# Moving the half-size Strassen step of a feed-forward chunk pair from the front of the chunk to its middle

## The chip, the cores and the metric

The kernel runs on one core of one Trainium2 chip. The metric is the device time of one execution in microseconds (us); less is better. The kernel before was run three times: 2200.41, 2201.24 and 2201.27 us, median 2201.24. The engines are named as in the profile: PE does matrix products (PEld is its weight load), DVE and ACT do element-wise work on 128-partition tiles, SP issues the transfers from device memory (HBM), and POOL does a few small things.

## The reference, cut to what matters

One decoder layer over 256 tokens of 2048 channels, all in float32. Two SwiGLU feed-forward blocks (FFN1 and FFN2, inner width 5504) stand around a mixer; the change touches only the first product of each feed-forward block.

```python
def swiglu(x, w_in, w_out):
    a, u = jnp.split(x @ w_in, 2, axis=-1)
    return (jax.nn.silu(a) * u) @ w_out

x = layer_norm(ALPHA * x + 0.5 * swiglu(x, ffn1_w_in[i], ffn1_w_out[i]), ln_g[i, 0], ln_b[i, 0])
...
x = layer_norm(ALPHA * x + 0.5 * swiglu(x, ffn2_w_in[i], ffn2_w_out[i]), ln_g[i, 2], ln_b[i, 2])
```

## The kernel before, in words

**Three passes.** A float32 product is made of three PE matrix products: weights and activations are each split into a high part and a remainder, and high x high (L1210), then high x remainder and remainder x high (both L1214) are added up in one PSUM bank. For the weights, ACT casts the loaded tile to its high part `wh` (L1141) and DVE subtracts it to get the remainder `wl` (L1153). One such pair (`wh`, `wl`) covers two k-tiles (a k-tile is 128 of the 2048 input channels) by 512 columns. In the feed-forward blocks there is room for six pairs (`NMAIN`). A pair is free again when PE has used it for the last time, so casts, and the splits behind them, can run at most six pairs ahead of PE.

**Chunk pairs.** In a feed-forward block, column chunk number 2 to 10 of the gate half and the same chunk of the up half make one `Quad`: two token tiles times two column slabs. With a low and a high block of k-tiles the four blocks of weights are called 11 (low k, gate), 12 (low k, up), 21 (high k, gate) and 22 (high k, up). A Quad takes k-tiles 0 to 7 by a Strassen-Winograd form with seven products in place of eight. It goes in two full steps: step 0 with low k-tiles 0, 1 and high 4, 5, and step 1 with 2, 3 and 6, 7. Each full step is seven elements: `11`, `t1`, `22`, `t3`, `t2`, `21`, `t4` (written `11.0` for step 0 and `11.1` for step 1). The four `t` elements are sums of weight blocks, added in place on DVE before the cast (L1119). Each element is one pair and serves two products, six matrix products on PE.

**The short step.** Chunks 2 to 9 of each feed-forward block (16 Quads, form "short") also take k-tile 8 as low and k-tile 9 as high by the same seven products: elements `h1`, `h2`, `h3`, `h4`. Their buffers are half as deep per block: `h1` reads a buffer of ring 11 that holds 11 and 22 side by side, `h2` is the sum of that buffer and a ring 21 buffer (12 and 21 side by side) written to a ring 12 buffer, `h3` is a half-size add, `h4` another. The k-tiles 10 to 15 are done plainly: elements `a0`..`a2` (gate) and `u0`..`u2` (up), each one pair that serves four products. Chunk 10 is a Quad of form "long" without a short step.

**Output units.** Between Quads stand two plain output units (`w_out` of the chunks of the group before), four pairs each; I call their eight pairs o1 to o8. Each pair serves four products.

**Rings.** Plain weight tiles come through a ring of four buffers (`raw`). The Strassen blocks come through rings of their own: two buffers for 11, one each for 12, 21 and 22 (`HIGH`). All loads go through SP's queue in one fixed order; a load waits there until its buffer is free. Ring 21's single buffer is freed by the add of `t4` (which takes the block 21 in) and, for the short step, by the split of `h4`. Ring 12's is freed by the splits of `t3` and of `h2`. `may_load` says which ring may load; its test on `shorted` keeps ring 12 empty until `h2` has been written to it.

**What sets the order.** `Quad.ORDER` (L87) is the order of a Quad's elements by hand: PE's products, the adds, casts and splits all follow it, through `feed` (L1166). When the program is built, a scheduler may move an instruction ahead of others on its engine, by its own estimate of when operands are ready; from then on every engine runs its list strictly as it stands. The number of PSUM banks for accumulation in these stages is seven (a Quad uses `p1` to `p7`).

Of the kernel before, what the change touches and what calls it, by code (L numbers as in the profile page):

```python
# [66 lines left out]
class Quad:  # L67
# [17 lines left out]
    SHORT = (8, 9)  # L85
    PLAIN = ((10, 11), (12, 13), (14, 15), (8, 9))
    ORDER = {  # L87
# [55 lines left out]
def hybrid_layer(ctx: ExitStack, tc: tile.TileContext, x, p, ln_g, ln_b, ffn1_w_in, ffn1_w_out, mix_w_in,  # L143
# [883 lines left out]
    for u in units:  # L1027
# [3 lines left out]
        if isinstance(u, Quad):  # L1031
            base = len(plan)
            for el in u.els:
# [3 lines left out]
                for key, ks, slab in el.get("load", ()):  # L1037
                    ring = key[2] if key else "raw"
                    if not key:
                        key = el["src"] = len(plan)  # L1040
# [43 lines left out]
    def may_load(ring):  # L1084
        if not loads[ring]:
            return False
        if ring == "raw":
            return taken["raw"] < NRAW
        key, kind = loads[ring][0][:2]
        if ring == "12" and not key[0].shorted:  # L1090
            return False
        return kind == region["kind"] and held["on"] and (held[ring] < HIGH[ring] or key in half)

# [72 lines left out]
    def feed():  # L1166
        while True:
            ring = min((r for r in loads if may_load(r)), key=lambda r: first_use[loads[r][0][0]], default=None)
            if ring:
                weight_dma(ring)  # L1170
            elif addable():
                weight_add()
            elif castable():
                weight_cast()
            elif cur["split"] < cur["cast"]:
                weight_split()
            else:
                return
# [141 lines left out]
```

## Time and profile before

| what | value |
|---|---|
| median of three runs | 2201.24 us |
| the profiled execution's own time | 2200.81 us |
| its span, first to last instruction | 2199.1 us |
| DVE busy | 1827.5 us (83%) |
| ACT busy | 1182.8 us (54%) |
| weight splits on DVE (L1153) | 975 instructions, 1140.9 us |
| weight casts on ACT (L1141) | 975 instructions, 975.9 us |
| weight adds on DVE (L1119) | 216 instructions, 254.7 us |
| granted PE clock | 0.998 over the span |

The span is what lies between the first and the last instruction; the execution's own time is 1.71 us more. "Busy" is a share over stages with different limits, so the stage of the change has to be looked at by itself. In a row of the timeline the first number is the start in us, the second the length, and a bracket at the end gives how long the engine was idle before the row and what it then waited for. A PE row's end is modelled: rows of 0.39 us that start 0.23 us apart are a full pipeline. Equal rows that follow each other are merged with a count, and then the length runs from the first start to the last end.

### The profile page before, as it was taken

The page shows a single profiled execution, that of the slowest core. Times are in us where ns is not written, and L with a number is a line of the kernel's source. Part 1 is how long each engine was busy: PE and PEld are TensorE (multiplying, and loading weights), DVE is VectorE, ACT ScalarE, POOL GpSimd, SP SyncE. Part 2 cuts the span into 40 slices and gives each one's busy share as a digit, 9 for nine tenths or more (in the row PEclk, how much of TensorE's full clock was granted, in tenths as well). Part 3 has the DMA queues.
Part 4 walks back from the last instruction along what each step waited for, and adds up shares of the span by engine and source line. Part 5 has one row for each costly group of instructions (what it writes and reads, how often), then busy time and mean ns, then how long its engine had stood idle before and what let it go on. Part 6 is the DMA issues. An engine that isn't in the chain of part 4 may idle for free.

```text
span 2199.1 us, 27091 instructions
## 1 busy us (share of the span) xinstructions
PE 2175.5 (99%) x9996; PEld 1811.4 (82%) x9996; DVE 1827.5 (83%) x2066; ACT 1182.8 (54%) x1412; POOL 20.0 (1%) x48
## 2 busy tenths in 40 slices
PE   9999999999999999999999999999999999999997
PEld 7988888888887888888888888798888888888886
DVE  6899999999886678657898888779999989998667
ACT  5555555555555534534565554645555555555463
POOL 1000000000000000000000000000000000000000
PEclk9999999999999999999999999999999999999999
DMA  8866666566663665554665676566666666665564
GB/s 263 265 193 200 210 204 194 186 201 211 208 194 116 197 216 178 185 181 153 220 203 177 202 244 210 171 210 201 192 200 189 203 211 201 201 210 176 192 221 144
DMA packets 228245, 436.29 MB, mean 198 GB/s; under 512 B 14608, under 2 KB 23312, under 8 KB 228112
## 3 DMA queue, kind: packets, MB, share of 16 engines
q1 hardware_dynamic: 226832, 430.37, 61.7%
q0 software_dynamic: 1280, 4.20, 0.5%
q8 instruction: 78, 1.28, 0.2%
q14 instruction: 55, 0.45, 0.1%
HBM read 430.31 MB, written 4.19 MB: 198 GB/s over the span
## 4 chain that ended last, share of the span: by engine, by line
PE 95%; DVE 2%; DMA 1%; ACT 1%; issue 1%; SPq 0%; DVEq 0%; ACTq 0%
PE bank L1214 61%; PE bank L1210 31%; PE bank L289 2%; PE bank L694 1%; DVE wl L1153 1%; DMA raw<-in_ffn_w_in_dram 1%; ACT wh L1141 1%; DMA raw<-in_ffn_w_out_dram 0%; DVE x L510 0%; DVE x L511 0%; PE bank L664 0%; ACT yT L490 0%; DVE x L496 0%; DVE raw L1119 0%; DVE bn L430 0%
## 5 line engine op out<-in xcount | busy, mean ns | idle before, releaser
L1141 ACT CAST wh<-raw 128x1024 fp32r<-128x1024 f32 (+2 forms) x975 | 975.9, 1030 | 763.0 <-PE bank L1214 331.3
L1153 DVE TENSOR_TENSOR wl<-raw,wh 128x1024 fp32r<-128x1024 f32 (+2 forms) x975 | 1140.9, 1197 | 237.1 <-ACT wh L1141 224.4
L1214 PE MATMUL bank<-wh,xl 128*128 128x512 f32 (+1 forms) x1624 | 625.6, 386 | 2.8 <-DVE xl L303 1.9
L1214 PE MATMUL bank<-wl,xh 128*128 128x512 f32 (+1 forms) x1624 | 625.9, 386 | 0.4 <-DVE wl L1153 0.4
L1210 PE MATMUL bank<-wh,xh 128*128 128x512 f32 (+1 forms) x1624 | 616.0, 387 | 0.4 <-ACT xh L302 0.4
L1214 PEld LDWEIGHTS bank<-wh,xl 128*128 128x128 f32 x1624 | 304.9, 188 | 63.3 <-DVE xl L303 4.0
L1210 PEld LDWEIGHTS bank<-wh,xh 128*128 128x128 f32 x1624 | 304.9, 188 | 58.9 <-ACT xh L302 1.5
L1214 PEld LDWEIGHTS bank<-wl,xh 128*128 128x128 f32 x1624 | 305.0, 188 | 58.6 <-DVE wl L1153 1.4
L1214 PE MATMUL bank<-wl,gh 128*128 128x512 f32 x896 | 348.5, 391 | 2.3 <-DVE wl L1153 2.3
L1214 PE MATMUL bank<-wh,gl 128*128 128x512 f32 x896 | 347.9, 390 | 0.0
L1210 PE MATMUL bank<-wh,gh 128*128 128x512 f32 x896 | 345.7, 392 | 0.0
L1119 DVE TENSOR_TENSOR raw<-raw,raw 128x1024 f32<-128x1024 f32 x216 | 254.7, 1180 | 12.4 <-DMA raw<-in_ffn_w_in_dram 6.7
L1214 PEld LDWEIGHTS bank<-wl,gh 128*128 128x128 f32 x896 | 168.3, 188 | 39.0 <-DVE wl L1153 4.8
L1210 PEld LDWEIGHTS bank<-wh,gh 128*128 128x128 f32 x896 | 168.1, 188 | 35.0 <-ACT wh L1141 0.4
L1214 PEld LDWEIGHTS bank<-wh,gl 128*128 128x128 f32 x896 | 168.2, 188 | 34.9
L1214 PE MATMUL bank<-wl,sh 128*128 128x512 f32 x464 | 181.6, 391 | 0.0
L1214 PE MATMUL bank<-wh,sl 128*128 128x512 f32 x464 | 180.5, 389 | 0.0
L1210 PE MATMUL bank<-wh,sh 128*128 128x512 f32 x464 | 177.1, 389 | 0.0
L1210 PEld LDWEIGHTS bank<-wh,sh 128*128 128x128 f32 x464 | 87.1, 188 | 18.3
L1214 PEld LDWEIGHTS bank<-wh,sl 128*128 128x128 f32 x464 | 87.1, 188 | 17.8
L1214 PEld LDWEIGHTS bank<-wl,sh 128*128 128x128 f32 x464 | 87.1, 188 | 17.8
L302 ACT CAST gh<-bank 128x512 fp32r<-128x512 f32 (+1 forms) x52 | 30.1, 578 | 75.9 <-PE bank L289 75.4
(184 smaller groups left out, 1121.5 us busy)
## 6 DMA issues: line engine op xcount, KB each, us to landing
raw<-in_ffn_w_in_dram SPq DMA_DIRECT2D x287, 512.0 KB, 4.4
raw<-in_mix_w_in_dram SPq DMA_DIRECT2D x176, 512.0 KB, 4.6
raw<-in_ffn_w_out_dram SPq DMA_DIRECT2D x168, 512.0 KB, 4.8
raw<-in_ffn_w_in_dram SPq DMA_DIRECT2D x66, 256.0 KB, 2.9
raw<-in_mix_w_out_dram SPq DMA_DIRECT2D x32, 512.0 KB, 4.7
raw<-in_ple_w_gate_dram SPq DMA_DIRECT2D x32, 512.0 KB, 4.9
raw<-in_ffn_w_in_dram SPq DMA_DIRECT2D x32, 384.0 KB, 4.0
raw<-in_branch_w_conv_dram SPq DMA_DIRECT2D x16, 512.0 KB, 5.1
```

The source lines that it names most:

```text
L289: state["turned"] = nc.tensor.transpose(tp[:, i * P : (i + 1) * P], src[:, i * P : (i + 1) * P], ident).ins
L302: state["half"] = nc.scalar.copy(hf, src).ins
L694: nc.tensor.matmul(gp[:, (h * 2 + t) * 64 : (h * 2 + t + 1) * 64], kd[:, h, t * P : (t + 1) * P], qd[:, h, t, :], start=True, stop=True)
L1119: nc.vector.tensor_tensor(out=out, in0=a, in1=b, op=ALU.add)
L1141: nc.scalar.copy(h[:, ks, :w], raw[:, ks, :w])
L1153: state["split"] = nc.vector.tensor_tensor(out=l[:, ks, :w], in0=raw[:, ks, :w], in1=h[:, ks, :w].bitcast(F32), op=ALU.subtract).ins
L1210: nc.tensor.matmul(acc, sh, wh[:, a, :n], start=first, stop=False)
L1214: nc.tensor.matmul(acc, x_part, w_part[:, a, :n], start=False, stop=last and i == 1)
```

## The change

The order of a short-form Quad is written anew. Before: `h1 u0 h2 h3 a0 h4`, then step 0 with `u1` and `a1`, then step 1 with `u2` and `a2`. Now: step 0 with `u0` and `a0`, then `u1 h1 h2 h3 a1 h4`, then step 1 as it was. The second edit lets ring 12 load block 12 of step 0 (`key[1]` is 0) at once; only step 1's waits until `h2` has been written. The products, adds, casts, splits and loads are the same in number and size.

```diff
@@ -85,7 +85,7 @@
     ORDER = {
-        "short": "h1 u0 h2 h3 a0 h4 11.0 u1 t1.0 22.0 t3.0 a1 t2.0 21.0 t4.0 11.1 u2 t1.1 22.1 t3.1 a2 t2.1 21.1 t4.1",
+        "short": "11.0 u0 t1.0 22.0 t3.0 a0 t2.0 21.0 t4.0 u1 h1 h2 h3 a1 h4 11.1 u2 t1.1 22.1 t3.1 a2 t2.1 21.1 t4.1",
@@ -1087,7 +1087,7 @@
-        if ring == "12" and not key[0].shorted:
+        if ring == "12" and key[1] and not key[0].shorted:
             return False
```

How the built program moves on DVE. All rows are from the third short Quad of FFN1 (chunk 4) and the output units behind it. `raw11`, `raw12`, `raw21` and `raw22` are buffers of the four rings, a bare `raw` is a buffer of the plain ring, L1119 rows are adds and L1153 rows are splits. Sizes end in x1024 for a pair and x512 for half of one.

First, the end of the Quad and the start of the output units, before:

```order
L1153 TENSOR_TENSOR wl_2122<-raw21_2007,wh_2121 128x1024
L535 TENSOR_TENSOR silu_2153<-silu_2153,bank6_87 128x512
L1119 TENSOR_TENSOR raw11_1830<-raw11_1830,raw21_2007 128x1024
L1153 TENSOR_TENSOR wl_2136<-raw11_1830,wh_2135 128x1024
L1119 TENSOR_TENSOR raw12_2309<-raw11_2019,raw21_2126 128x1024
L1153 TENSOR_TENSOR wl_2148<-raw_1927,wh_2147 128x1024
L1153 TENSOR_TENSOR wl_2163<-raw_1978,wh_2162 128x1024
L1119 TENSOR_TENSOR raw21_2126<-raw12_2309,raw11_2019 128x512
L1153 TENSOR_TENSOR wl_2181<-raw_2043,wh_2180 128x1024
L1153 TENSOR_TENSOR wl_2193<-raw_2095,wh_2192 128x1024
```

and in the changed program:

```order
L1153 TENSOR_TENSOR wl_2123<-raw21_2016,wh_2122 128x1024
L535 TENSOR_TENSOR silu_2154<-silu_2154,bank2_83 128x512
L1119 TENSOR_TENSOR raw11_1936<-raw11_1936,raw21_2016 128x1024
L1153 TENSOR_TENSOR wl_2136<-raw11_1936,wh_2135 128x1024
L1153 TENSOR_TENSOR wl_2149<-raw_1948,wh_2148 128x1024
L1153 TENSOR_TENSOR wl_2164<-raw_2004,wh_2163 128x1024
L1153 TENSOR_TENSOR wl_2182<-raw_2045,wh_2181 128x1024
L1153 TENSOR_TENSOR wl_2194<-raw_2096,wh_2193 128x1024
```

Behind the split of `t4.1` stood the next Quad's `h2` add, ahead of the splits of o1 and o2, and its `h3` add ahead of o3; now o1 to o4 follow at once.

Second, around the end of step 0 (the add and split of `t4.0`), before:

```order
L1153 TENSOR_TENSOR wl_2003<-raw21_1897,wh_2002 128x1024
L1119 TENSOR_TENSOR raw11_1651<-raw11_1651,raw21_1897 128x1024
L1153 TENSOR_TENSOR wl_2016<-raw11_1651,wh_2015 128x1024
L1153 TENSOR_TENSOR wl_2029<-raw11_1830,wh_2028 128x1024
L1153 TENSOR_TENSOR wl_2040<-raw_1827,wh_2039 128x1024
L1119 TENSOR_TENSOR raw11_1830<-raw11_1830,raw12_1966 128x1024
```

and in the changed program, down to the split of `h4`:

```order
L1153 TENSOR_TENSOR wl_1919<-raw21_1639,wh_1918 128x1024
L1119 TENSOR_TENSOR raw11_1475<-raw11_1475,raw21_1639 128x1024
L1153 TENSOR_TENSOR wl_1933<-raw11_1475,wh_1932 128x1024
L1119 TENSOR_TENSOR raw12_1950<-raw11_1651,raw21_1923 128x1024
L1153 TENSOR_TENSOR wl_1945<-raw_1795,wh_1944 128x1024
L1153 TENSOR_TENSOR wl_1959<-raw11_1651,wh_1958 128x1024
L1119 TENSOR_TENSOR raw21_1923<-raw12_1950,raw11_1651 128x512
L1153 TENSOR_TENSOR wl_1978<-raw12_1950,wh_1977 128x1024
L1153 TENSOR_TENSOR wl_1990<-raw21_1923,wh_1989 128x1024
L1153 TENSOR_TENSOR wl_2001<-raw_1807,wh_2000 128x1024
L1119 TENSOR_TENSOR raw21_1923<-raw21_1923 128x512
L1153 TENSOR_TENSOR wl_2013<-raw21_1923,wh_2012 128x512
```

The Quad's own `h2` add now stands directly behind the split of `t4.0`, and reads a ring 21 buffer (raw21_1923) whose load could start only when `t4.0`'s add had released that ring; the splits of `u1` and `h1` stand behind it.

Third, the end of the output units, in the changed program:

```order
L1153 TENSOR_TENSOR wl_2318<-raw_2215,wh_2317 128x1024
L1119 TENSOR_TENSOR raw11_1963<-raw11_1963,raw12_2084 128x1024
L303 TENSOR_TENSOR gl_2246<-bank0_81,gh_2245 128x512
L535 TENSOR_TENSOR silu_2199<-silu_2199,h_2200 128x512
L1119 TENSOR_TENSOR raw12_2084<-raw12_2084,raw22_2087 128x1024
L1153 TENSOR_TENSOR wl_2356<-raw11_1963,wh_2355 128x1024
```

Here, behind the split of the next Quad's `u0`, stand now the adds of its `t1.0` and `t3.0`. Before, no L1119 row stood between the split of `u0` and the splits of `h2` and `h3`, which were summed earlier.

## The prediction, on record before the changed kernel was run

> **What bounds the kernel now.** I read the page first, then PE's waits over the whole span and in the two feed-forward stretches, then two periods (one Quad and two output units) engine by engine, and last the DVE timeline around the places that the change touches.
>
> ```profile
> span 2199.1 us, 27091 instructions
> PE 2175.5 (99%) x9996; PEld 1811.4 (82%) x9996; DVE 1827.5 (83%) x2066; ACT 1182.8 (54%) x1412; POOL 20.0 (1%) x48
> PE 95%; DVE 2%; DMA 1%; ACT 1%; issue 1%; SPq 0%; DVEq 0%; ACTq 0%
> PE bank L1214 <- DVE wl L1153: 2.7, 6, 0.8
> PE bank L1214 <- DVE wl L1153: 1.0, 2, 0.8
> PE bank L1214 <- DVE wl L1153: 0.8, 2, 0.5
> 207.44:268.90 61.46, 61.20 (x274) 50.29 (x273) 56.02 (x57) 34.09 (x38) 0.00 (x0) 1.00 0.66 206
> 397.76:460.63 62.87, 62.87 (x283) 52.02 (x281) 57.46 (x59) 34.85 (x39) 0.00 (x0) 1.00 0.64 203
> ```
>
> The chain lies on PE for 95% of the span. The fourth line is PE's wait for weight remainders in the whole run (us, times, longest), the fifth and sixth the same from 80 to 600 us and from 1470 to 1990 us, where all 16 short Quads lie: 1.0 and 0.8 us. The last two lines are windows (length, then busy time of PE, PEld, DVE, ACT, POOL). In the later one PE has no hole, and DVE works 57.46 of 62.87 us: PE sets the pace and DVE has 5.41 us to spare. In the earlier one DVE spares as much, but PE does wait: DVE's slack is in the wrong place.
>
> What PE loses is more than the profile's idle figure, since rows of 0.39 us start 0.23 us apart: 0.16 us of each wait hides under a modelled end.
>
> ```profile
> 186.63 0.39 PE L1214 MATMUL bank<-wh,xl 128*128 128x512 f32 x1
> 187.77 0.50 PE L1214 MATMUL bank<-wl,gh 128*128 128x512 f32 x1 [0.75 <-DVE wl L1153]
> 1764.79 0.39 PE L1214 MATMUL bank<-wh,xl 128*128 128x512 f32 x1
> 1765.16 0.50 PE L1214 MATMUL bank<-wl,gh 128*128 128x512 f32 x1
> ```
>
> The first pair starts 1.14 us apart, a loss of 0.91. The second, 0.37 apart, loses 0.14 and shows no idle at all. Four waits of 1.8 us together plus 4 x 0.16, plus that fifth, make **2.6 us** lost in the 16 short Quads. All five read `gh` behind `xl`: the first product of o1, just behind a Quad.
>
> **The change, part by part.** I measure a lead: PE's first product with a remainder minus the end of its split. First the third Quad of FFN1, one of the lean ones, where PE waits, then a steady one:
>
> ```profile
> 225.17 1.22 DVE L1119 TENSOR_TENSOR raw<-raw,raw 128x1024 f32<-128x1024 f32 x1
> 227.58 3.50 DVE L1153 TENSOR_TENSOR wl<-raw,wh 128x1024 fp32r<-128x1024 f32 x3 [1.19 <-ACT wh L1141]
> 241.96 1.22 DVE L1119 TENSOR_TENSOR raw<-raw,raw 128x1024 f32<-128x1024 f32 x1
> 244.35 1.23 DVE L1153 TENSOR_TENSOR wl<-raw,wh 128x1024 fp32r<-128x1024 f32 x1 [1.17 <-ACT wh L1141]
> 246.06 1.23 DVE L1119 TENSOR_TENSOR raw<-raw,raw 128x1024 f32<-128x1024 f32 x1 [0.49 <-DMA raw<-in_ffn_w_in_dram]
> 247.20 2.35 DVE L1153 TENSOR_TENSOR wl<-raw,wh 128x1024 fp32r<-128x1024 f32 x2
> 249.47 0.68 DVE L1119 TENSOR_TENSOR raw<-raw,raw 128x512 f32<-128x512 f32 x1
> 233.32 0.39 PE L1214 MATMUL bank<-wl,xh 128*128 128x512 f32 x1
> 246.92 0.39 PE L1214 MATMUL bank<-wl,xh 128*128 128x512 f32 x1
> 248.47 0.50 PE L1214 MATMUL bank<-wl,gh 128*128 128x512 f32 x1 [0.27 <-DVE wl L1153]
> ```
>
> In order on DVE: the add of t4.0, its split with those of 11.1 and u2, the add and split of t4.1, the next Quad's h2 add, o1 and o2, the h3 add. An add must be followed by its own cast before its split can run, hence the 1.19 and 1.17. The split of 11.1 ends at 227.58 + 1.14 + 1.22 = 229.94: lead 3.38. That of t4.1 ends at 245.58: lead 1.34. That of o1 ends at 248.42 and PE stands waiting: lead 0.05.
>
> ```profile
> 415.83 3.49 DVE L1153 TENSOR_TENSOR wl<-raw,wh 128x1024 fp32r<-128x1024 f32 x3 [1.19 <-ACT wh L1141]
> 432.67 1.23 DVE L1153 TENSOR_TENSOR wl<-raw,wh 128x1024 fp32r<-128x1024 f32 x1 [1.17 <-ACT wh L1141]
> 434.36 1.22 DVE L1119 TENSOR_TENSOR raw<-raw,raw 128x1024 f32<-128x1024 f32 x1 [0.46 <-DMA raw<-in_ffn_w_in_dram]
> 435.50 2.35 DVE L1153 TENSOR_TENSOR wl<-raw,wh 128x1024 fp32r<-128x1024 f32 x2
> 422.51 0.39 PE L1214 MATMUL bank<-wl,xh 128*128 128x512 f32 x1
> 436.12 0.39 PE L1214 MATMUL bank<-wl,xh 128*128 128x512 f32 x1
> 437.25 0.39 PE L1214 MATMUL bank<-wl,gh 128*128 128x512 f32 x1
> ```
>
> The same leads here: 4.32, 2.22 and 0.53.
>
> *Removed at the end of a Quad.* The h2 add (1.14 from start to start) with its 0.49 wait for the load leaves the place ahead of o1. In the lean Quad o1's split comes 0.43 too late (the last row's 0.27 and the hidden 0.16); 1.63 sooner, it would be 1.2 us early.
>
> *Added behind t4.0.* The same add with the same kind of wait: its addend's buffer is released by t4.0's add as formerly by t4.1's.
>
> ```profile
> 243.24 2.74 SPq L1077 DMA_DIRECT2D raw<-in_ffn_w_in_dram  x3
> raw<-in_ffn_w_in_dram SPq DMA_DIRECT2D x4, 256.0 KB, 2.8
> raw<-in_ffn_w_out_dram SPq DMA_DIRECT2D x8, 512.0 KB, 4.8
> ```
>
> SP issued the two halves at 243.24, 0.06 after the add ended (241.96 + 1.22), and they had landed 2.8 us later; DVE reaches the add 2.3 us after the release. The wait repeats at about 0.49, and 1.63 us come ahead of the split that follows t4.0's (now u1, then 11.1). Its lead falls to 3.38 - 1.63 = 1.75 in the lean Quad and 4.32 - 1.60 = 2.7 in the steady one. Both stay positive, so PE sees nothing: it lives on the pairs already split. Behind the waiting add stand u1, h1 and the h3 add; if the lead were gone, each microsecond of wait would cost PE one.
>
> *Moved inside the Quad.* Up to t4.1's split DVE now does the h2 and h3 adds (1.14, and 0.60: rows overlap by 0.08) with the 0.49 wait, and no longer the adds of t1.0 and t3.0 (2 x 1.14), done ahead of the Quad. The h4 add loses the work that stood between it and its split:
>
> ```profile
> 211.09 0.69 DVE L1153 TENSOR_TENSOR wl<-raw,wh 128x512 fp32r<-128x512 f32 x1 [0.76 <-ACT wh L1141]
> 456.31 3.94 DVE L1153 TENSOR_TENSOR wl<-raw,wh 128x1024 fp32r<-128x1024 f32 x3 [1.00 <-ACT wh L1141]
> 253.41 1.22 DVE L1153 TENSOR_TENSOR wl<-raw,wh 128x1024 fp32r<-128x1024 f32 x1 [0.39 <-ACT wh L1141]
> ```
>
> The first row is h4's split, which in the lean Quad waits 0.76 already; in a steady one (no such row there) it will come new. The sum is 2.23 - 2.28 = -0.05, up to +0.71 with that wait. t4.1's lead becomes 0.6 to 1.4 in the lean Quad and 1.5 to 2.3 in the steady one. The adds of t1.0 and t3.0 fill time at the end of the output units: in the steady period DVE idles there 1.00 us anyway (second row, waiting for a free pair). In the lean one DVE reaches that place sooner by the 2.2 us of h2, h3 and wait. Should the cover be gone, 2.28 us a period come off the lead.
>
> *o5.* Its load starts when o1's split frees a plain buffer, and DVE already waits 0.39 for it through its cast (third row). With no adds between o1 and o5 that wait grows, at most by the 1.75 us of adds; o5's lead is larger than o1's, since each output pair feeds PE for four products, 12 x 0.227 = 2.72 us, and costs DVE 1.14.
>
> *The `may_load` edit* adds no transfer; it lets 12.0 be there for t1.0. Without it that add could not come before h2. Casts, products and bytes stay as they are.
>
> **Sum.** At o1 the lean Quads gain 1.6 less 0 to 0.7, so the five stalls can go: -2.6. Over the lean periods the added waits (0 to 0.76 at h4, some tenths at o5) eat part of what DVE carries from one Quad to the next; I take 0.5 back: **-2.1 us**. Ends: -2.6, and 0 if all of it is eaten. The profiled execution took 2200.81 us: 2199.1 - 2.1 = 2197.0 of span, 2198.7 with the 1.71 around it. It stood 0.43 below the median of the runs, so I forecast **2199.1 us**, 0.1% less.
>
> **The rivals.** *No gain:* the stalls move to t4.1 or h4, ends within 0.5 us of 2201.2. For it: the same adds and the same kind of wait are all still there. Against: leads of 1.7 and more where they go.
>
> *Slower:* the load for h2's add lands late at its new place, in the middle of step loads. It decides once the wait exceeds the lead less the add: 3.38 - 1.14 = 2.2 us in the lean Quads, 4.32 - 1.14 = 3.2 in steady ones. If landing takes twice as long as seen, 5.6 us, the wait is 3.3; six lean Quads (I take the first three of each block) lose 1.1 each and ten steady ones 0.1: +7.6, less 2.6, is +5.0: 2206.2 us. For it: output loads do take 4.8 us (row above). Against: 2.8 for this load at a place just as full.
>
> *Faster by more than the stalls:* PE's weight loads fill 52.02 of 62.87 us in the steady period. If a twentieth of the other 10.85 us were holes of the order's making, 0.54 x 16 = 8.7 us could go: 2192.5. Against it: PE's own rows fill the whole window and start 0.23 us apart. The Trainium skill, "Perfetto Trace Analysis", section "Identifying the Most-Contended Engine", says that matmul busy time is no good measure of what is left on the tensor engine and that the weight load's busy share is; by it this rival would be the likely one. The even start spacing here says otherwise.
>
> **How the numbers follow.** Forecast 0.66, no gain 0.20, slower 0.10, much faster 0.04. This kernel's measurement can tell about 0.2%, 4.4 us, from no change. The first two cases lie inside it, so: faster 0.05 (0.04 and a sliver of the forecast), same 0.85, slower 0.10. The range goes from 2197.6 (all stalls gone, with a microsecond of scatter) to 2203.6 (halfway to the slower rival).
>
> **What would show it.** Right: no PE wait for `wl` at o1 in the 16 Quads; on DVE an idle of about 0.5 us for an `in_ffn_w_in` load behind t4.0's split, and none behind t4.1's; an idle near 0.76 ahead of every h4 split. Wrong: PE waiting for `wl` with `xh` or `sh` operands in mid-Quad, that load wait above 2 us, or periods longer than 62.87 us in steady stretches; a period shorter than that would speak for the last rival.

## The result, and the profile after

The changed kernel took 2218.55 us (median of four runs, 2216.71 to 2219.84), the one before 2201.26 beside it. The ratio is 1.008, with a 95% interval of 1.0068 to 1.0092: **slower by 17.3 us**. That is 0.8%. I had forecast 2199.1 us, with a range that ended at 2203.6.

The page of the changed kernel: span, busy time by engine, and the share of each engine in the chain of waits that ended last.

```profile
span 2218.1 us, 27095 instructions
PE 2185.6 (99%) x9996; PEld 1808.8 (82%) x9996; DVE 1823.4 (82%) x2066; ACT 1177.7 (53%) x1412; POOL 19.4 (1%) x48
PE 61%; DVE 21%; DMA 7%; issue 7%; ACT 3%; DVEq 0%; SPq 0%; ACTq 0%
```

DVE has no more work than before (1823.4 against 1827.5 us), but the chain now runs over DVE, DMA and ACT for 31% of the span, where it lay on PE for 95%.

PE's waits of the changed kernel, from 80 to 600 us and from 1470 to 1990 us (us in total, times, longest):

```profile
PE bank L1210 <- ACT wh L1141: 4.1, 10, 0.8
PE bank L1210 <- ACT wh L1141: 5.9, 14, 0.9
```

PE no longer waits for a remainder (`wl`) at o1, or anywhere else in these stretches. It waits for high parts (`wh`): its list has the first product of some pairs ahead of the last products of the pair before, so a late pair now shows on its cast. Two such places per steady Quad are the rows below, on PE's timeline:

```profile
482.17 0.39 PE L1210 MATMUL bank<-wh,xh 128*128 128x512 f32 x1
482.58 0.50 PE L1210 MATMUL bank<-wh,sh 128*128 128x512 f32 x1
...
505.90 0.41 PE L1210 MATMUL bank<-wh,xh 128*128 128x512 f32 x1
506.75 0.73 PE L1210 MATMUL bank<-wh,gh 128*128 128x512 f32 x2 [0.45 <-ACT wh L1141]
```

Starts 0.41 and 0.85 us apart instead of 0.23. Added up over all PE rows, the time from start to start beyond 0.227 us is 27.9 us before and 47.4 us after. The difference, 19.4 us, is all of the 19.0 by which the span grew.

**One steady period.** From the split of t1.1 in one Quad to that in the next; the window's columns are its length, then busy time of PE, PEld, DVE, ACT, POOL. The changed kernel:

```profile
430.83:494.84 64.01, 63.68 (x284) 52.06 (x283) 56.94 (x59) 34.42 (x39) 0.00 (x0) 1.00 0.64 198
```

Every steady period (I compare four in each block, behind the first three, which are the lean ones) is now 63.5 to 64.5 us long, against 62.87 in six of the eight before (62.6 to 63.2 in all). DVE works 56.94 us of it and idles 7.07. What it waits for, in that window, and below it what ACT's casts wait for when they wait for a free pair:

```profile
DVE wl L1153 <- ACT wh L1141: 6.4, 5, 3.0
DVE raw L1119 <- DMA raw<-in_ffn_w_in_dram: 0.5, 1, 0.5
ACT wh L1141 <- PE bank L1214: 0.3, 1, 0.3
```

The same rows of the kernel before, from 358.79 to 421.66 us:

```profile
DVE wl L1153 <- ACT wh L1141: 5.0, 6, 1.7
DVE raw L1119 <- DMA raw<-in_ffn_w_in_dram: 0.4, 1, 0.4
ACT wh L1141 <- PE bank L1214: 4.8, 4, 1.6
```

This is a good short reading of the case. Before, the casts stood 4.8 us a period waiting for PE to release a pair: work was ready ahead of PE. After, 0.3 us in this period (0.8 on average over the eight steady ones): hardly anything is ahead any more. The DVE waits say little until one asks of each what its own cast had waited for:

| DVE idle in one steady period, us | before | after |
|---|---|---|
| its own add, then the cast, then the split, or a cast queued behind such a one (a chain) | 2.36 | 3.48 |
| a load | 0.84 | 3.55 |
| a free pair (PE is behind) | 2.14 | 0 |

Waits under 0.1 us are left out. Only the last row was time to spare. The rows of DVE's timeline that carry the rise, in the changed kernel at o1 to o5 and from t4.0 to 11.1:

```profile
442.92 4.62 DVE L1153 TENSOR_TENSOR wl<-raw,wh 128x1024 fp32r<-128x1024 f32 x4
447.46 0.68 DVE L535 TENSOR_TENSOR silu<-h,bank 128x512 f32<-128x512 f32 x1
451.18 1.23 DVE L1153 TENSOR_TENSOR wl<-raw,wh 128x1024 fp32r<-128x1024 f32 x1 [3.04 <-ACT wh L1141]
...
478.42 1.23 DVE L1153 TENSOR_TENSOR wl<-raw,wh 128x1024 fp32r<-128x1024 f32 x1 [1.19 <-ACT wh L1141]
480.15 1.22 DVE L1119 TENSOR_TENSOR raw<-raw,raw 128x1024 f32<-128x1024 f32 x1 [0.51 <-DMA raw<-in_ffn_w_in_dram]
...
489.21 0.69 DVE L1153 TENSOR_TENSOR wl<-raw,wh 128x512 fp32r<-128x512 f32 x1 [0.76 <-ACT wh L1141]
490.16 2.36 DVE L1153 TENSOR_TENSOR wl<-raw,wh 128x1024 fp32r<-128x1024 f32 x2 [0.26 <-ACT wh L1141]
```

o1 to o4 are split one behind the other (442.92), and then DVE idles 3.04 us ahead of o5 (451.18). The same place before:

```profile
437.77 0.68 DVE L1119 TENSOR_TENSOR raw<-raw,raw 128x512 f32<-128x512 f32 x1
438.37 2.35 DVE L1153 TENSOR_TENSOR wl<-raw,wh 128x1024 fp32r<-128x1024 f32 x2
440.64 0.68 DVE L535 TENSOR_TENSOR silu<-h,bank 128x512 f32<-128x512 f32 x1
441.82 1.22 DVE L1153 TENSOR_TENSOR wl<-raw,wh 128x1024 fp32r<-128x1024 f32 x1 [0.51 <-ACT wh L1141]
```

Between o1's split, which frees the buffer for o5's load, and o5 itself DVE had one add, h3's (437.77); h2's add stood ahead of o1's split.

Over the eight steady periods compared, this wait went from 0.45 us on average (0.20 to 0.98) to 3.18 (2.68 to 3.65).

### The profile page after: what moved, and what is told of

Its sections match the earlier page's. It is cut to its first block, busy times and chain, and to the rows that moved or that the text cites. A ratio compares the mean times of both kernels' runs of the same rounds, so it can differ in the third digit from the quotient of the medians.

```text
span 2218.1 us, 27095 instructions
## 1 busy us (share of the span) xinstructions
PE 2185.6 (99%) x9996; PEld 1808.8 (82%) x9996; DVE 1823.4 (82%) x2066; ACT 1177.7 (53%) x1412; POOL 19.4 (1%) x48
## 4 chain that ended last, share of the span: by engine, by line
PE 61%; DVE 21%; DMA 7%; issue 7%; ACT 3%; DVEq 0%; SPq 0%; ACTq 0%
PE bank L1214 39%; PE bank L1210 19%; DVE wl L1153 11%; DVE raw L1119 5%; DMA raw<-in_ffn_w_out_dram 4%; DMA raw<-in_ffn_w_in_dram 3%; ACT wh L1141 3%; DVE silu L535 1%; PE bank L289 1%; DVE x L600 1%; PE bank L694 1%; DVE gl L303 1%; DVE h L535 1%; DVE x L597 0%; DVE x L510 0%
## 5 line engine op out<-in xcount | busy, mean ns | idle before, releaser
L1153 DVE TENSOR_TENSOR wl<-raw,wh 128x1024 fp32r<-128x1024 f32 (+2 forms) x975 | 1141.5, 1198 | 263.4 <-ACT wh L1141 252.2
L1210 PEld LDWEIGHTS bank<-wh,xh 128*128 128x128 f32 x1624 | 304.8, 188 | 62.1 <-ACT wh L1141 4.3
L1119 DVE TENSOR_TENSOR raw<-raw,raw 128x1024 f32<-128x1024 f32 x216 | 254.6, 1179 | 14.7 <-DMA raw<-in_ffn_w_in_dram 7.3
L600 DVE TENSOR_TENSOR x<-x,bank 128x512 f32<-128x512 f32 x64 | 43.5, 679 | 12.9 <-PE bank L1214 12.9
```

Source lines behind the costliest of these rows:

```text
L600: nc.vector.tensor_tensor(out=xc, in0=xc, in1=acc, op=ALU.add)
L1119: nc.vector.tensor_tensor(out=out, in0=a, in1=b, op=ALU.add)
L1153: state["split"] = nc.vector.tensor_tensor(out=l[:, ks, :w], in0=raw[:, ks, :w], in1=h[:, ks, :w].bitcast(F32), op=ALU.subtract).ins
L1210: nc.tensor.matmul(acc, sh, wh[:, a, :n], start=first, stop=False)
```

## The theories

Three went into the experiments. In the texts that were put on record before the runs, VectorE is DVE, TensorE is PE and ScalarE is ACT. **Theory 1**, DVE's pace: DVE's idle time no longer fits. Its first form was that the adds of h2 and h3 had been filler between o1 and o4 while o5's load was on its way, and that the new wait at o5 is what costs the time. Its second form, made after the first four runs, is a budget: the waits for chains and loads, added up over a period, must fit into what DVE's work leaves of PE's 62.87 us, and it does not matter which of them is removed. **Theory 2** is my recorded rival: the wait of h2's add for its load, in mid-Quad. **Theory 3**: PE's waits for casts, where its list has a product too early. The kernels below ran with the one before beside them (medians of 2200.8 to 2201.2 us).

## Take the adds from between o1 and o4, in the kernel before

```diff
-        nc.vector.tensor_tensor(out=out, in0=a, in1=b, op=ALU.add)
+        with tc.issue_after(state["split"]) if short in ("h2", "h3") else nullcontext():
+            nc.vector.tensor_tensor(out=out, in0=a, in1=b, op=ALU.add)
```

> The kernel before, with one thing changed: the adds of h2 and h3 may not run before the last split that stands ahead of them, so VectorE can no longer put them between the splits of o1 to o4; they come behind the split that opens the next Quad, and nothing else is moved. Theory 1 (VectorE's pace: those adds were work for VectorE while o5's load was on its way; without them it idles there, and its slack of about 5 us a period is used up): VectorE's wait ahead of o5's split grows from 0.5 to 2 us or more, the periods grow from 62.9 to 63.5 to 64.1 us, and the time is 2208 to 2220 us. Theory 2 (the wait of h2's add for its load, 0.5 us in mid-Quad, costs the time): no such wait is in mid-Quad here, 2199 to 2203 us. Theory 3 (TensorE's waits for casts behind the moved step): the step stands where it stood, 2199 to 2203 us.

Measured: **2197.25 us**, ratio 0.9983 (0.9973 to 0.9992): faster than the kernel before, and below what any of the three theories had said. The wait at o5 did grow, and nothing was lost. DVE's rows at o5 and at the end of the output units, and ACT's row in front of the second:

```profile
438.77 1.23 DVE L1154 TENSOR_TENSOR wl<-raw,wh 128x1024 fp32r<-128x1024 f32 x1 [2.03 <-ACT wh L1142]
...
455.81 2.59 DVE L1154 TENSOR_TENSOR wl<-raw,wh 128x1024 fp32r<-128x1024 f32 x2 [1.80 <-ACT wh L1142]
```

```profile
454.72 1.05 ACT L1142 CAST wh<-raw 128x1024 fp32r<-128x1024 f32 x1 [5.75 <-PE bank L1215]
```

2.03 us at o5, and still 1.80 us at h2, where the cast had waited for a free pair. So the longer wait at o5 is paid for out of time that DVE had to spare, and the first form's time was wrong by more than 10 us. The adds were filler only in small part: over the eight steady periods the wait grew from 0.45 to 2.42 us, of which h3's add is 0.6; the rest is the load itself, ready for o5's cast 5.4 us after the end of o1's split on average, where it had been 4.0. The run also removes the stalls at o1: with no add in front of o1's split, PE waits for no remainder in the feed-forward stretches.

## Take away the wait for h2's load, in the changed kernel

```diff
-        made["h2"] = dict(src=two, add=(one, three), short="h2", behind=-1, free=[two],
+        made["h2"] = dict(src=two, add=(one, one), short="h2", behind=-1, free=[two],
```

> The changed kernel, but h2's add reads the buffer of the one loaded k-tile twice and leaves out the other addend (another sum is computed, with the same instructions), so that it need not wait for the load that it waited 0.51 us for behind t4.0. Theory 2 (this wait is the cause): the whole loss of 17 us is gone, 2199 to 2203 us. Theory 1 (VectorE's pace, with about 2.3 us of new idle ahead of o5's split and 0.5 at h2): each removed 0.5 us comes off each of 16 periods, at most 8 us: 2210 to 2216 us, and the wait ahead of o5 stays at 2 us or more. Theory 3 (TensorE waits for the casts of high halves): no change, 2216 to 2220 us.

Measured: 2211.51 us, ratio 1.0048 (1.0033 to 1.0063). The wait is gone from h2's add and stands, at 0.3 to 0.5 us, ahead of h3's, which needs the same load; o5's is still 2 to 3.5 us in all periods but one. A steady period of it:

```profile
425.96:489.61 63.65, 63.55 (x283) 51.81 (x282) 56.85 (x59) 34.22 (x39) 0.00 (x0) 1.00 0.63 198
```

0.4 us less than in the changed kernel. 7 us is what theory 1 allowed, and theory 2 wanted all 17 back. But the wait for this load has moved more than gone, so this run alone does not refute theory 2; the cover for t4.0 and t4.1 below does. Over the eight steady periods a period is 0.65 us shorter, 0.35 of it at o5; why that wait shrank was not followed up.

## A fifth buffer for plain tiles, in both kernels

To make room, one slab of operand halves fewer is kept and one difference operand serves two channel blocks, so both kernels compute other numbers, with one cast and one split of 512 columns fewer in each block.

```diff
...
+    def extra_free(kind):
+        return not extra and region["kind"][:3] == "ffn" and kind == region["kind"] and taken["raw"] >= NRAW
...
-            raw = rp.tile([P, KG, CC], F32, tag="raw", name="raw", bufs=NRAW)
-            taken["raw"] += 1
+            if extra_free(kind):
+                raw = region["pool"].tile([P, KG, CC], F32, tag="rawx", name="raw", bufs=1)
+                extra.add(key)
+            else:
+                raw = rp.tile([P, KG, CC], F32, tag="raw", name="raw", bufs=NRAW)
+                taken["raw"] += 1
```

> The changed kernel with a fifth buffer for plain k-tile pairs inside the feed-forward blocks, so that o5's load is issued one split earlier. To make room, one slab of operand halves fewer is kept and the difference operand of channel block 3 is not made (that of block 2 is used for both: other numbers, the same TensorE work, one cast and one split of 512 columns fewer per block). Theory 1 (VectorE runs out of loaded k-tiles at o5): its wait of 2.85 us ahead of o5's split falls under 1 us, the periods fall from 64.0 to 64.5 us to 62.9 to 63.2 us, and the time is 2198 to 2204 us. Theory 2 (h2's load) and theory 3 (casts): the wait at h2 and the casts stand where they stood, 2214 to 2220 us.

> The control for the fifth buffer: the same edit on the kernel before (the difference operand of channel block 2 is used for block 3 too). Theory 1: VectorE's waits at o5 to o8 are 0.4 to 0.7 us there and PE sets the pace, so little changes: 2197 to 2202 us; the five PE stalls of together 2.6 us at o1 may shrink. Theories 2 and 3: the same.

Measured: 2206.71 us in the changed kernel, ratio 1.0025 (1.0015 to 1.0034), and 2197.48 in the one before, 0.9986 (0.9977 to 0.9996). In the changed kernel the wait moved from o5 to o6 and fell to 1.2 to 2.4 us, and the steady periods came to PE's floor:

```profile
425.58:488.31 62.73, 62.73 (x282) 51.94 (x281) 56.94 (x59) 35.07 (x39) 0.00 (x0) 1.00 0.64 203
```

12 of the 17 us come back; 9 us stay between it and its control. They are lost in the lean Quads, where PE still waits for casts in both blocks. This is nearer to theory 1 than to the others, and with the first experiment it gave the second form: one wait made shorter is as good as another.

## Let a split cover the casts of t4.0 and t4.1, in the changed kernel

The budget's test: leave o5 as it is and remove something else.

```diff
-                "t4": dict(src=k11, add=(k11, k21), behind="t2 21", use=[("p4", 1, hi)], drop=[k21], free=[k11]),
+                "t4": dict(src=k11, add=(k11, k21), behind="t2" if short else "t2 21", use=[("p4", 1, hi)], first=short,
+                           **(dict(free=[k11, k21]) if short else dict(drop=[k21], free=[k11]))),
...
-        nc.vector.tensor_tensor(out=out, in0=a, in1=b, op=ALU.add)
+        add = nc.vector.tensor_tensor(out=out, in0=a, in1=b, op=ALU.add).ins
+        state["first"] = add if el.get("first") else None
...
-            with gated("lo"):
+            with tc.issue_after(state["first"]) if state.get("first") else gated("lo"):
```

> The changed kernel; in short Quads the add of t4.0 now stands ahead of 21.0's split and that of t4.1 ahead of 21.1's, so that VectorE has this split to do while ScalarE casts the sum. Nothing else of the order is set by hand (h2's add comes to stand behind u1's split). Theory 1 in its second form (a budget: VectorE's waits that nothing can shift, added up over one period of a Quad and two output units, must fit into the some 5.4 us that its work leaves of the 62.87 us that TensorE needs; in the changed kernel they were 1.2 at t4.0, 0.5 at h2, 1.0 at h4 and 11.1, 1.2 at t4.1 and 2.9 at o5, 6.8 us in all): with some 2 us of it gone the sum fits, steady periods fall from 64.0 to 62.9 to 63.2 us though the wait at o5 stays at 2 to 3 us; 2198 to 2208 us, less the nearer the three lean Quads of a block come to the floor. Theory 1 in its first form (the wait at o5 itself is what costs the time): 2213 to 2219 us. Theory 3 (TensorE's waits for casts at u1 and o1): no more than 2 us off, 2215 to 2220 us.

Measured: **2197.06 us**, ratio 0.998 (0.9971 to 0.999). All of the loss is back, and 4 us more. DVE at o5, and around t4.0 (399.95 is its add, then come 21.0, t4.0 and u1):

```profile
375.57 1.23 DVE L1155 TENSOR_TENSOR wl<-raw,wh 128x1024 fp32r<-128x1024 f32 x1 [2.82 <-ACT wh L1143]
...
399.95 1.23 DVE L1120 TENSOR_TENSOR raw<-raw,raw 128x1024 f32<-128x1024 f32 x1
401.10 3.64 DVE L1155 TENSOR_TENSOR wl<-raw,wh 128x1024 fp32r<-128x1024 f32 x3
405.14 1.23 DVE L1120 TENSOR_TENSOR raw<-raw,raw 128x1024 f32<-128x1024 f32 x1 [0.41 <-DMA raw<-in_ffn_w_in_dram]
```

o5's wait is as long as in the changed kernel, 2.82 us here and 1.6 to 4.2 over all periods, and h2's is still there too; the 1.19 at t4.0 is gone, that at t4.1 down to 0.14. The period, and the casts' wait for a free pair in it:

```profile
356.12:418.98 62.86, 62.86 (x283) 52.01 (x282) 57.40 (x59) 35.49 (x39) 0.00 (x0) 1.00 0.63 201
```

```profile
ACT wh L1143 <- PE bank L1217: 5.2, 9, 1.7
```

PE has no hole, and pairs are ready ahead of it again (5.2 us of waiting, 0.3 in the changed kernel). PE waits nowhere in the two feed-forward stretches, though nothing was set in its own order: theory 3 falls, its waits were the symptom. Theory 2 falls too, since the wait of h2's add stands as it was, and so does theory 1 in its first form. Above PE's 0.227 us per row, all rows together lose 24.1 us here, 3.8 less than before.

## Cover h4's cast as well

```diff
-        made["h4"] = dict(src=three, add=(three, three), short="h4", behind=at("h3"), free=[three],
+        made["h4"] = dict(src=three, add=(three, three), short="h4", behind=at("h3"), free=[three], first=True,
```

> As the run before, and h4's add also stands ahead of a1's split, so that this covers h4's cast too (0.76 and 0.26 us of VectorE's waits in steady Quads). Theory 1 as a budget: the steady periods are at TensorE's floor already, so only what the three lean Quads of a block still lose can come back: 0 to 4 us below the run before, 2197 to 2206 us. Theory 1 in its first form: 1 us a period below the run before, if that is far above 2201 us. Theory 3: as the run before.

Measured: 2197.04 us, ratio 0.9981 (0.9972 to 0.999): the same as without it, as the budget says of a sum that fits already. DVE's wait at 11.1 grew from 0.3 to 0.9 us or so; from ACT's row one sees why that costs nothing, the cast had waited for a free pair:

```profile
413.31 1.05 ACT L1143 CAST wh<-raw 128x1024 fp32r<-128x1024 f32 x1 [0.91 <-PE bank L1217]
```

## Cover h4's cast alone

The edit of the last run on the changed kernel, with the adds of t4.0 and t4.1 held behind the splits of 21.0 and 21.1.

> The changed kernel, where h4's add stands ahead of a1's split and nothing else is helped (the adds of t4.0 and t4.1 are held behind the splits of 21.0 and 21.1, as they were; ahead of t4.1's split a bias-and-gate operation of 0.68 us now comes behind the add). Budget: h4's wait of 0.76 us goes, but 11.1's cast is queued behind h4's on ScalarE and its wait grows from 0.26 to 0.9 us, so that this gains about 0.1 us; t4.1's wait falls from 1.17 to 0.6 us. The sum falls from 6.8 to 6.1 us a period, steady periods to 63.3 to 63.5 us, the time to 2205 to 2212 us. If each wait counted by itself (0.76 + 0.6 us): 2196 to 2200 us; if only o5's: 2216 to 2220 us.

Measured: 2198.58 us, ratio 0.9989 (0.998 to 0.9999). I expected 2205 to 2212, and missed. I had carried the 0.9 us at 11.1 over from the run above without asking what its cast waits for. DVE's rows from t4.0 on, and from a1 through h4 and 11.1:

```profile
469.23 1.23 DVE L1156 TENSOR_TENSOR wl<-raw,wh 128x1024 fp32r<-128x1024 f32 x1 [1.19 <-ACT wh L1144]
...
477.58 0.69 DVE L1121 TENSOR_TENSOR raw<-raw 128x512 f32<-128x512 f32 x1
478.19 4.16 DVE L1156 TENSOR_TENSOR wl<-raw,wh 128x1024 fp32r<-128x1024 f32 x4
```

Where DVE is late there is no wait for a free pair, and both waits go: 0.76 and 0.26, and in most steady periods 0.6 at t4.1. With 1.6 us less the idle sum is 5.1 to 6.3 us, and steady periods are 62.1 to 63.3 us long. The budget stands and my entry in it was wrong. With this alone the changed kernel is no longer behind the one before. The time also lies in the range of "each wait counted by itself"; what speaks against that reading is the run before this one, where h4's 0.76 us went as well and nothing was gained.

## Give DVE more work, in the kernel before

One split per short Quad (22.1's) is done once or three times more.

```diff
+            made["22.1"]["again"] = 1
...
+            for _ in range(el.get("again", 0)):
+                state["split"] = nc.vector.tensor_tensor(out=l[:, ks, :w], in0=raw[:, ks, :w],
+                                                         in1=h[:, ks, :w].bitcast(F32), op=ALU.subtract).ins
```

> The kernel before, where VectorE does 22.1's split twice in every short Quad (the same values twice): 1.14 us more of its work in each of 16 periods, no wait or load added. Theory 1 as a budget: in steady periods before, VectorE still waits some 1.7 us a period at h2 for a free pair of buffers, which is what is left of its slack, so 1.14 us is taken from that and costs nothing there: 2200 to 2206 us, with what is lost lost in the lean Quads. Theories 2 and 3: no change, 2200 to 2203 us.

> The kernel before, where VectorE does 22.1's split four times in every short Quad: 3.4 us more of its work in each of 16 periods. Theory 1 as a budget: the 1.7 us are used up and the other 1.7 us are added to each period, 16 x 1.7 = 27 us: 2218 to 2235 us, with steady periods of 64 to 65 us and TensorE's waits at one or two places after the added work. Theories 2 and 3 (only a late load or a late cast costs time): at most the one stall that the late splits make in each Quad before VectorE has caught up, 2200 to 2210 us.

Measured: 2209.0 us, ratio 1.0034 (1.0022 to 1.0046), and 2231.49 us, 1.0135 (1.012 to 1.015). A steady period with one more split, and with three more:

```profile
362.96:425.96 63.00, 63.00 (x283) 51.94 (x282) 58.37 (x60) 35.16 (x39) 0.00 (x0) 1.00 0.63 201
```

```profile
432.67:497.85 65.18, 63.46 (x281) 51.59 (x280) 60.76 (x63) 34.72 (x39) 0.00 (x0) 1.00 0.61 194
```

1.14 us more cost a steady period 0.13 us; 3.42 us more cost 2.31. The first microsecond is free, and behind it all is paid (2.28 us more work, 2.18 us longer): a threshold, as a budget has one, though 1.1 us high and not the 1.7 I had read from one wait. In the lean Quads there is little such reserve. There the one split cost 0.6 to 1.8 us a period, in part through stalls at o1:

```profile
PE bank L1218 <- DVE wl L1154: 3.7, 3, 1.3
```

(80 to 600 us; 1.0 in the kernel before.) That is why the first of the two ended 3 us above its range. With three more splits DVE still waits at h2, h3 and a0 for free pairs, 0.9 to 1.6 us a period, while PE stalls further on. So the sum over a period is a bound and not the whole rule: six pairs is as far ahead as DVE can work, and spare time at one place does not all help another.

## Work put into the wait at o5, in the changed kernel

o4's split, the one ahead of the wait, is done twice.

```diff
+                if kind[:3] == "ffn" and after_short[-1] + 3 == i:
+                    plan[i]["again"] = 1
```

> The changed kernel, where VectorE does o4's split twice behind each short Quad (the same values twice): 1.14 us more of its work in each of 16 periods, put where it waits 2.9 us for o5's load. If the adds of h2 and h3 were filler there before (work that costs nothing while the load is on its way), this work costs nothing either: o5's wait falls from 2.9 to 1.8 us and the time stays at 2216 to 2221 us. If VectorE's work counts wherever it stands: 16 x 1.14 = 18 us more, 2233 to 2238 us.

Measured: 2224.27 us, ratio 1.0108 (1.0093 to 1.0123): 5.7 us above the changed kernel, between the two expectations. In the steady periods it is as the first expectation says: the work fills the wait. A period, and the added split with the wait behind it:

```profile
433.21:497.00 63.79, 63.35 (x283) 51.89 (x282) 58.17 (x60) 34.42 (x39) 0.00 (x0) 1.00 0.62 199
```

```profile
449.95 1.23 DVE L1160 TENSOR_TENSOR wl<-raw,wh 128x1024 fp32r<-128x1024 f32 x1
451.09 0.68 DVE L535 TENSOR_TENSOR silu<-h,bank 128x512 f32<-128x512 f32 x1
453.39 1.23 DVE L1157 TENSOR_TENSOR wl<-raw,wh 128x1024 fp32r<-128x1024 f32 x1 [1.62 <-ACT wh L1145]
```

The wait is 1.62 and the periods are 63.5 to 64.4 us long, no longer than the changed kernel's. Lost are 0.7 to 1.9 us in four of the lean periods, and 1.6 between the blocks. What exactly is late there I did not follow up.

## The same cover in the kernel before

The edit to t4.0 and t4.1, in the kernel before.

> The kernel before with the same edit to the adds of t4.0 and t4.1 that brought the changed kernel to 2197 us (each ahead of the split of 21.0 or 21.1). If the place of the short step is worth something by itself, this kernel stays above the changed kernel with that edit, at 2200 to 2202 us, with the stalls at o1. If what counts is only that VectorE's budget and its leads hold, both places come out alike at TensorE's floor: 2196.5 to 2198.5 us, without stalls at o1 and with steady periods of 62.87 us.

Measured: 2197.31 us, ratio 0.9983 (0.9974 to 0.9993), beside 0.998 (0.9971 to 0.999) for the changed kernel with it. The stalls at o1 are gone from this one as well, and the steady periods are 62.87 us. **Where the short step stands makes no measurable difference by itself.** Either place reaches the same floor once DVE's waits fit.

## Why o5's load is late, in the changed kernel

The SP queue issues three loads for the next Quad just ahead of those for o5 to o8. Here they are held until o8's is issued.

```diff
+    def held_back(key, kind):
+        return kind[:3] == "ffn" and not isinstance(key, int) and key[1:] in ((0, "21"), ("h", "11"))
...
+            with tc.issue_after(state["load"]) if held_back(key, kind) else nullcontext():
+                state["load"] = nc.sync.dma_start(raw[:, at + ks.start : at + ks.stop, :width], src[:, ks, :]).ins
...
+        if held_back(key, kind) and loads["raw"] and loads["raw"][0][0] < key[0].base:
+            return False
```

> The changed kernel, where three loads for the next Quad (21.0 and the two halves of h1's buffer), which its SP queue issues just ahead of the loads for o5 to o8, are held until o8's load is issued. In the changed kernel o5's cast began 6.0 us after o1's split had ended, in the one before 4.1 us. If the transfers that run just ahead are what makes o5's load late, this comes back to 4.1 us, VectorE's wait at o5 falls from about 3 to about 1.1 us, the sum of its waits for chains and loads from 6.8 to 5 us, under the 5.4 us of room, and the time to 2197 to 2203 us. If o5's load is late only because its four neighbours are issued closer together: 5.5 to 6 us again, 2215 to 2220 us.

Measured: 2207.47 us, ratio 1.0027 (1.0017 to 1.0037). ACT's row of o5's cast in the kernel before, in the changed one, and here:

```profile
440.74 1.05 ACT L1141 CAST wh<-raw 128x1024 fp32r<-128x1024 f32 x1 [4.30 <-DMA raw<-in_ffn_w_out_dram]
```

```profile
450.10 1.05 ACT L1141 CAST wh<-raw 128x1024 fp32r<-128x1024 f32 x1 [4.56 <-DMA raw<-in_ffn_w_out_dram]
```

```profile
446.66 1.05 ACT L1147 CAST wh<-raw 128x1024 fp32r<-128x1024 f32 x1 [2.52 <-DMA raw<-in_ffn_w_out_dram]
```

From the end of o1's split (436.72, 444.14 and 442.73 us) that is 4.0, 6.0 and 3.9 us; over the eight steady periods it is 4.0, 6.1 and 4.1 on average. What SP issued around it, before and in the changed kernel (three loads for the next Quad, then those for o5 to o8):

```profile
431.57 2.73 SPq L1077 DMA_DIRECT2D raw<-in_ffn_w_in_dram  x3
436.74 4.37 SPq L1077 DMA_DIRECT2D raw<-in_ffn_w_out_dram  x4
```

```profile
440.68 3.17 SPq L1077 DMA_DIRECT2D raw<-in_ffn_w_in_dram  x3
444.16 3.78 SPq L1077 DMA_DIRECT2D raw<-in_ffn_w_out_dram  x4
```

Both kernels issue three such loads first. Before, they were issued 5.2, 4.8 and 2.8 us ahead of o5's, and only the last was still under way then (it landed 0.6 us later). In the changed kernel they were issued 3.5, 1.1 and 0.7 us ahead, and all three were under way (they landed 0.1, 1.8 and 2.4 us later). With h2's add and its wait gone from there, o1's split follows t4.1's directly, and the loads that the two release are bunched. The transfers just ahead are what made the load late, about 2 us of it. DVE's wait at o5 falls to 0.8 to 2.0 us in steady periods, but in most of them o6 or o7 now waits 0.1 to 1.1 us, and the lean Quads keep their stalls. That is why 11 us came back and not all 17.

## Why the prediction was wrong

**The step that failed** is the one on o5, and with it the sum. I wrote that the wait at o5 grows "at most by the 1.75 us of adds", entered it as "some tenths at o5", and took 0.5 us back for all added waits. Measured, it grew by 2.7 us a period (0.45 to 3.18). The direction was right; the size was off fivefold or more, and the bound counted the wrong thing. Of the 1.75 us of adds only h3's, 0.6 us, stood between o1's split and o5; h2's add stood ahead of o1's split and could not cover the load. The other 2.1 us are the load itself, ready 6.1 us after o1's split and no longer 4.0. I had taken its landing as given. Holding the three transfers ahead of it back brought it to 4.1 and the time down by 11 us. Taking the adds away in the kernel before made the load late as well (5.4 us, and a wait of 2.0 to 3.1 us).

**What made the size matter** was the reading of DVE's slack. I wrote that DVE works 57.46 of 62.87 us and "has 5.41 us to spare". In the period of the table 3.2 of it were already taken by chains and loads, and 2.1 were to spare (the added splits found 1.1 of it free). The change added 1.1 at h4 and 11.1 (I had 0.76) and 2.7 of loads. That is 3.8 against 2.1, so each period had to grow by up to 1.7; it grew by 1.14, with 0.42 us less of DVE's busy time in the window. The lean Quads had less to spare from the start: in the earlier window, of which I wrote that DVE "spares as much", 1.0 of its 5.44 us of idle time was a wait for a free pair, and in the first two periods of FFN1 none was. There an added wait counts in full. The six lean periods grew by 12.8 us together, the eight steady ones by 9.9; the stretch between the blocks became 2.8 shorter.

**The leads** followed from it. I let u1 and 11.1 start from the leads of before and come down to 1.75 to 2.7, t4.1 to 0.6 to 2.3. But a lead is only carried over if DVE regains it before the next Quad. In the steady period of the changed kernel u1's was 0.4 and t4.1's 0.3 us.

**What was right.** No PE wait for `wl` at o1 is left, and the 2.6 us there were real: the five kernels that fit end 3.4 to 4.0 us below the one before. The wait of h2's add stayed what it had been, 16 waits of 7.3 us together and 0.8 at most, so the *slower* rival as I put it did not happen; the loss came through a place that I had only in a clause. h4's 0.76 came as foreseen; 11.1's 0.26, its cast queued behind h4's, did not. Of my signs of being wrong only the longer steady periods came. My three signs of being right all came too: they tested the moves that I had listed, and not the wait at o5 on which the sum failed.

**The much faster rival** falls too. Five kernels without PE waits there end within 0.5 us of each other, at 2197.0 to 2197.5, and their full steady periods are 62.87 us with PEld busy for 52.0, as before. The Trainium skill, "Perfetto Trace Analysis", section "Identifying the Most-Contended Engine", would have the share of peak arithmetic and the weight load's busy share measure what is left; nothing here got under the even spacing of PE's own rows. The same section takes busy share as a fair measure for the vector engine. By it DVE would have had 11% left in the steady period of the changed kernel. The trace shows nothing left: at 56.94 of 64.01 us (89%) DVE set the pace, because the rest was chains and loads.

## What to carry to other kernels

Before idle time of an engine is counted as spare, ask of each wait what the instruction ahead of it had waited for: only waits for a free buffer, on the consumer's side, are spare; a chain or a load is as good as work. Add up these hard waits over one period, before and after an edit, and compare them with what the pacing engine leaves. A load's landing is no constant in that sum: ask what is issued just ahead of it. One number hints at the state, how long the producers wait for free buffers (4.8, 0.8 and 7.6 us a steady period before, after and with t4.0 and t4.1 covered). It is no clean sign: it was 2.5 with three added splits, at 65.2 us a period, and 2.7 with h4's cast alone covered, at 62.7. And where the sum does not fit, the cheapest wait to remove need not be the one that the edit made: moving an add ahead of an independent split, at two places in each Quad, was enough.

## What was not expected of the hardware

The same 512 KB load, issued when o1's split ended, was ready for its cast after 4.0 or 6.0 us, with one or three other loads of the same queue still under way when it was issued. The Trainium skill, "SBUF — State Buffer", section "The DMA setup-cost knee", gives a fit of 2 us plus the bytes over 436 kB per us; by it such a load by itself would take an estimated 3.2 us. No run here shows it alone; with other transfers beside it, such a load landed 3.6 to 7.2 us after it could start, over the steady periods of all runs.
